# Selecting keys for the last four query blocks: in the projection, or beside the trunk

## The chip, the cores and the metric

One core of one Trainium2 chip runs the whole program. The metric is the device time of one execution in microseconds, as the median of several runs. The engines are called as in the profile: PE (TensorE, matmuls; PEld its weight loads), DVE (VectorE), ACT (ScalarE), POOL (GpSimd) and SP (SyncE, whose queue issues nearly all DMAs here).

## What is computed

A decoder layer with 2048 tokens and a width of 1024, in float32 (matmuls of full precision are made of three products of rounded halves). Three mixers work on columns of one projection, then an output projection, a norm, a gated feed-forward of width 2816 and a second norm:

```python
z = x @ w_in                      # columns split among the three mixers
# A: for each query, the 256 keys with the highest index score are attended to
rel   = relu(einsum('bqhd,bsd->bqhs', qi, ki) * IDX_DIM ** -0.5)
score = where(key_pos <= t, einsum('bqhs,bqh->bqs', rel, wi), -inf)
_, sel = top_k(score, 256)        # then softmax attention over sel
# B: differential attention, C: three dilated windows
x = LN(alpha * x + concat(A, B, C) @ w_o)
x = LN(alpha * x + (silu(x @ w_gate) * (x @ w_up)) @ w_down)
```

The change touches only where and when `sel` is found for the last of the sixteen blocks of 128 queries.

## The kernel before

The 2048 queries are 16 blocks of 128 (`NB`); groups `g` of 512 rows are the unit of the projection and of the trunk.

**Projection.** Four sections (two parts, two halves of the rows) run over chunks of 128 output columns. `chunk` makes a tile of 24 matmuls (`pj`, L543 to L545), ACT and DVE split it into halves `st` (L565 to L569), SP stores it. Value columns, with tokens down the rows, go through `natural` (`pnv`, `pnc`, L593 to L595). Weight pieces `w` are loaded by SP and split by ACT and POOL, the last six by ACT and DVE.

**Selection.** `index_work` handles two query blocks. It scores them against all earlier keys (for each 512 columns and each of four heads two matmuls `is`, L366 and L367, a relu on ACT, a multiply-add on DVE, L370 and L373), stores the scores, finds a threshold by 13 bisection passes (for even blocks on DVE, L399; for odd ones on ACT, L392), and finishes with a chain of a mask on ACT, some ten DVE instructions and one of POOL (L330) for each block. The result is a mask `sel` in DRAM. Width grows with the block: block 12 has 1664 columns, block 15 has 2048. The generators yield estimated costs for DVE, ACT, POOL and, while scoring, PE. In the projection `Background(2)` runs two of them at a time: `pump` is called between matmuls, advances them by planned time and keeps, in `free`, how long each of the three engines is taken. When five chunks are left, `bg.drain()` emits all that remains, and the pool `tk` with keys and scores is closed.

**`general_select`** then adds the flags of all blocks, loads the sum on every engine and branches: only if a flag was set, a slow exact selection runs. Nothing of it ran in the profile but the branch (L452). After it come the distance table of C and, with three chunks left, the loads of C's first head (`c_load`).

**Branch C with attention of group 0**, then the **trunk**. The trunk is woven of two streams. The main one is, for each group of 512 rows, `head` (transposes `mt`, output projection `wo`, norm, `xt`) and `body` (six rounds of gate `fg`, up `fu` and down `fd`, by `mm3`, L1215 to L1217; results to DVE, `sg`, `h`, `rT`). The side one is `all_attention`: attention of groups 1, 2 and 3 (A and B), then `head(3)`. Groups 2 and 3 are run A first, then B in one lane. Main group g starts after `ready` says that attention g has been emitted, and group 3's body needs all of `head(3)`. `weave` chooses who emits next: `due` rises by each cost of the side stream and falls by `share` times each cost of the main one; the side goes when `due` is below zero, or when the main stream sleeps. A yield's second number is a time to sleep in the planner's clock, which each cost of PE advances. PSUM in the trunk: three banks `f`, two `lg`, one `tr`, two `ac`. The order of emission is the priority; the framework fixes each engine's order when the program is built, and takes the branch as one indivisible unit.

Of the kernel before, what the change touches and what calls it, by code (L numbers as in the profile page):

```python
# [21 lines left out]
P = 128  # L22
# [17 lines left out]
OB2, UP_BUFS, CTB = 2, 4, 2  # L40
DRAIN, HEAD = 5, 3
C_EVAC = (1, 3)
LAM0 = 0.8 - 0.6 * math.exp(0.0)
# [23 lines left out]
C_SHARE = 0.2  # L67
T_SHARE = (0.45, 0.45, 0.45, 0.45)
T_AHEAD = 4.0
# [25 lines left out]
def tile_hybrid_layer(  # L95
# [212 lines left out]

    tk, close_tk = pool("tk", "right")
    kih = tk.tile([P, S], F32R, name="kih")  # L310
    kil = tk.tile([P, S], F32R, name="kil")
    dv = tk.tile([P, S], BF16, name="dumpv")
    da = tk.tile([P, S], BF16, name="dumpa")
    sign = tk.tile([P, S], BF16, name="sign")

    def index_keys(g):
        t0 = g * 512
        for dst, src in ((kih, kid[0]), (kil, kid[1])):
            load(dst[:, t0:t0 + 512].bitcast(F32), src[:, t0:t0 + 512])

# [16 lines left out]

    def index_work(blocks):


        n = len(blocks)
        q0 = blocks[0]
# [11 lines left out]
        for i, qb in enumerate(blocks):  # L354
# [5 lines left out]
            for c0 in range(0, w, 512):  # L360
                m = min(512, w - c0)
                acc = s_[:, c0:c0 + m]
                for h in range(4):
                    pt = bank("mm", f"is{qb}_{c0}_{h}")
                    q_ = qs[:, h, i * P:(i + 1) * P]
# [72 lines left out]

    def general_select():

        gp, close = pool("gp", "right")
        nf = gp.tile([P, 1], F32, name="nf")
        ones = gp.tile([P, 1], F32, name="ones")
        fi = gp.tile([1, 1], I32, name="fi")
        V.tensor_reduce(nf, flags, axis=AX.X, op=ALU.add)
        V.memset(ones, 1.0)
        pt = bank("ac", "nflags")
        PE.matmul(pt[:1, :1], nf, ones, start=True, stop=True)
# [3 lines left out]
        with tc.If(nc.values_load(fi[:1, :1]) > 0):  # L452
            for qb in range(2, NB):
                w = (qb + 1) * P
# [208 lines left out]
    def advance(loads, n):  # L663
        for _ in range(n):
            if loads:
# [3 lines left out]
                else:  # L669
                    xts[loads[0][0]] = tl  # L670

    xts = {}
    loads = [((0, g), read_x(0, g)) for g in range(2)]
    advance(loads, 5)
    for n, (part, half) in enumerate(sections):
        for pair in LISTS[part]:
            wts = None
            for g in (2 * half, 2 * half + 1):
# [4 lines left out]
                if pair == ("v",):  # L683
                    flush()
                    wts = wts or ws.take(3)
                    for tb, pt in enumerate(natural((3, 3, 2), 324, tl, f"v{g}", wts)):
# [7 lines left out]
                        store(vbd[:, b * P:(b + 1) * P, :].rearrange("h t d -> t h d"), vst.bitcast(F32))  # L694
                    for b0 in range(max(2, 4 * g), 4 * g + 4, 2):
                        bg.add(index_work([b0, b0 + 1]))
                    left -= 1
# [9 lines left out]
                else:  # L707
                    wts = wts or ws.take(len(pair))
                    for w_, what in zip(wts, pair):
                        chunk(w_, what, t0, tl)  # L710
                        left -= 1
                        last = n == 3
                        store_some(8 if last else 4)
                        if left == DRAIN:
                            bg.drain()
                            close_tk()
                            general_select()
                            cq, close_cq = pool("cq", "right")
                            ctab = c_distances(cq)
                            lambdas(cq)  # L720
                        if left == HEAD:
                            heads = {0: c_load(0)}
                        if what == 2:
                            flush()
                            index_keys(g)
                        advance(loads, 1)
# [687 lines left out]
    last, turns = [], [0]  # L1414

    def all_attention():

        for g in range(1, 4):
            yield from attention(g)
            ready[0] = g  # L1420
        hp, close_hp = pool("hp", "right")
        last.extend((hp, close_hp))
        last.append((yield from head(3, hp, Stream(hp, [w_o[dc] for dc in range(8)], 2, 2, "g"), iter(()), H_TAGS)))
# [77 lines left out]
```

## Time and profile before

| | us |
|---|---|
| median of 3 runs (3476.6 to 3488.01) | 3483.5 |
| the profiled execution | 3468.75 |
| its span, first to last instruction | 3467.0 |
| PE busy (mean granted clock 0.959 of full) | 3160.0 |
| DVE busy | 2148.0 |
| ACT busy | 1661.7 |
| POOL busy | 1020.6 |

The projection ends at about 695 us of the span, branch C at about 1160, the trunk's third body at about 3060; the last body runs alone to the end. Busy time of PE is the union of matmuls whose ends are modelled; a matmul of 512 columns is listed with 0.39 us, though one starts each 0.227 us in a dense stretch. A clock of 1.00 is the full one.

### The profile page before, as it was taken

Reading aid. Unit: us, or ns where it says so; the run is one execution under the profiler, and the core shown is the slowest. Engines: PE = TensorE matmul, PEld = TensorE weight load, DVE = VectorE, ACT = ScalarE, POOL = GpSimd, SP = SyncE. Lnnn points to the kernel's source line nnn. Section 1 sums busy time; section 2 is a strip of 40 time slices with the busy share of each in tenths; the row PEclk is TensorE's granted clock in tenths of the full one; section 3 lists DMA queues with packets and bytes.
Section 4 is the critical chain, followed back from the end, with each engine's and each line's share of the span. In section 5 each row is a group of like instructions: output and inputs, shape, how many; then the busy total and the mean of one; then the engine's idle time right before and its main releaser. Section 6 shows DMA issues by size and latency. Waiting matters only on the chain. (4 is left out here: it accounts for less than half of the span.)

```text
span 3467.0 us, 45777 instructions
## 1 busy us (share of the span) xinstructions
PE 3160.0 (91%) x15994; PEld 2601.1 (75%) x15994; DVE 2148.0 (62%) x5367; ACT 1661.7 (48%) x3113; POOL 1020.6 (29%) x591
## 2 busy tenths in 40 slices
PE   8998889869889799989988999999889999999997
PEld 7776667758878678877776777777678778778885
DVE  4979699547788567655468656465866555363224
ACT  3756656447666355545443445354444454232222
POOL 3221313014223123232223323321333332343332
PEclk9999999979999799999999999999999999999999
DMA  7453645588764633242244332422434242433322
GB/s 220 159 179 132 206 156 172 173 197 193 179 164 127 196 90 101 89 116 66 81 125 128 108 99 79 127 56 77 139 98 112 78 118 70 138 101 91 103 86 84
DMA packets 261241, 434.78 MB, mean 125 GB/s; under 512 B 49680, under 2 KB 149520, under 8 KB 256656
## 3 DMA queue, kind: packets, MB, share of 16 engines
q1 hardware_dynamic: 257808, 427.65, 42.4%
q0 software_dynamic: 1120, 3.67, 0.4%
q8 instruction: 126, 2.06, 0.2%
q14 instruction: 107, 0.88, 0.1%
q10 hardware_dynamic: 2080, 0.52, 0.1%
HBM read 331.65 MB, written 100.11 MB: 125 GB/s over the span
## 5 line engine op out<-in xcount | busy, mean ns | idle before, releaser
L155 POOL TENSOR_TENSOR f<-fr,f 128x1024 fp32r<-128x1024 f32 (+2 forms) x320 | 570.3, 1783 | 1400.6 <-ACT f L154 1314.4
L154 ACT CAST f<-fr 128x1024 fp32r<-128x1024 f32 (+2 forms) x392 | 321.4, 820 | 486.5 <-PE fd L1217 166.1
L1217 PE MATMUL fd<-h,f 128*128 128x512 f32 x704 | 280.7, 399 | 9.2 <-POOL f L155 9.0
L1215 PE MATMUL fd<-h,f 128*128 128x512 f32 x704 | 283.4, 403 | 3.1 <-ACT f L154 3.1
L1215 PE MATMUL fg<-xt,f 128*128 128x512 f32 x704 | 283.7, 403 | 0.7 <-ACT f L154 0.3
L1217 PE MATMUL fg<-xt,f 128*128 128x512 f32 x704 | 279.9, 398 | 3.4 <-DVE f L155 2.8
L1215 PE MATMUL fu<-xt,f 128*128 128x512 f32 x704 | 280.8, 399 | 1.4 <-ACT f L154 1.4
L1216 PE MATMUL fd<-h,f 128*128 128x512 f32 x704 | 279.9, 398 | 1.2 <-DVE h L155 1.2
L1217 PE MATMUL fu<-xt,f 128*128 128x512 f32 x704 | 278.4, 395 | 2.1 <-DVE f L155 1.2
L1216 PE MATMUL fg<-xt,f 128*128 128x512 f32 x704 | 280.0, 398 | 0.2 <-POOL xt L155 0.2
L1216 PE MATMUL fu<-xt,f 128*128 128x512 f32 x704 | 277.7, 394 | 0.0
L543 PE MATMUL pj<-xt,w 128*128 128x512 f32 x544 | 220.6, 406 | 25.6 <-ACT w L154 8.9
L545 PE MATMUL pj<-xt,w 128*128 128x512 f32 x544 | 217.8, 401 | 1.4 <-POOL w L155 1.4
L544 PE MATMUL pj<-xt,w 128*128 128x512 f32 x544 | 218.1, 401 | 0.7 <-POOL xt L155 0.7
L1022 ACT ACTIVATE c<-c,ob 128x256 f32<-128x256 f32 (+1 forms) x384 | 172.6, 451 | 66.4 <-DVE ob L1016 62.6
L1338 DVE TENSOR_TENSOR sg<-sg,fu 128x512 f32<-128x512 f32 x88 | 60.3, 686 | 228.3 <-PE fu L1217 227.6
L1352 DVE TENSOR_TENSOR rT<-rT,fd 128x512 f32<-128x512 f32 x160 | 109.3, 685 | 146.8 <-PE fd L1217 146.0
L1217 PEld LDWEIGHTS fd<-h,f 128*128 128x128 f32 x704 | 134.1, 190 | 41.5 <-POOL f L155 15.2
L155 POOL TENSOR_TENSOR w<-wr,w 128x1024 fp32r<-128x1024 f32 (+2 forms) x42 | 99.3, 2369 | 221.2 <-ACT w L154 200.9
L1217 PEld LDWEIGHTS fg<-xt,f 128*128 128x128 f32 x704 | 133.2, 189 | 33.0 <-DVE f L155 4.8
L1215 PEld LDWEIGHTS fd<-h,f 128*128 128x128 f32 x704 | 134.3, 191 | 30.2 <-ACT f L154 5.3
L1217 PEld LDWEIGHTS fu<-xt,f 128*128 128x128 f32 x704 | 132.3, 188 | 31.4 <-DVE f L155 2.8
(815 smaller groups left out, 8229.3 us busy)
## 6 DMA issues: line engine op xcount, KB each, us to landing
fr<-in_w_gate_dram SPq DMA_DIRECT2D x88, 512.0 KB
fr<-in_w_up_dram SPq DMA_DIRECT2D x88, 512.0 KB
fr<-in_w_down_dram SPq DMA_DIRECT2D x128, 256.0 KB
wr<-in_w_in_dram SPq DMA_DIRECT2D x42, 512.0 KB
fr<-in_w_o_dram SPq DMA_DIRECT2D x24, 512.0 KB
fr<-in_w_down_dram SPq DMA_DIRECT2D x64, 192.0 KB
ocd<-ob SPq DMA_DIRECT2D x16, 528.0 KB
ot<-ocd SPq DMA_DIRECT2D x32, 264.0 KB
```

The costliest lines, as they stand in the source:

```text
L154: A.copy(hi, src)
L155: lo_eng.tensor_tensor(lo, src, hi.bitcast(F32), op=ALU.subtract)
L543: PE.matmul(pt, wv[:, 0, k], tl[0][:, k], start=(k == 0), stop=False)
L544: PE.matmul(pt, wv[:, 0, k], tl[1][:, k], start=False, stop=False)
L545: PE.matmul(pt, wv[:, 1, k], tl[0][:, k], start=False, stop=(k == KC - 1))
L1022: A.activation(nl, nl, AF.Exp, bias=ob[:, place(blk), 64:65], scale=-1.0, accum_out=ob[:, place(blk), 65:66])
L1215: PE.matmul(pt, wv[:, 0, k], hi[:, k], start=(k == 0), stop=False)
L1216: PE.matmul(pt, wv[:, 0, k], lo[:, k], start=False, stop=False)
L1217: PE.matmul(pt, wv[:, 1, k], hi[:, k], start=False, stop=(k == n - 1))
L1338: V.tensor_tensor(sg, sg, pt, op=ALU.mult)
L1352: V.tensor_tensor(d, d, pt, op=ALU.add)
```

## The change

`LATER = 12`: the projection queues `index_work` only for blocks 2 to 11. Keys and buffers are made by a new `index_tiles`, once as `tk` for the projection, once as `lk` for the trunk. A generator `late_selection` loads the keys again from DRAM, makes two lanes (blocks 12 and 13; 14 and 15) and runs them in the side stream between attention 1 and attention 2; each lane sleeps for the longest of its engines' declared costs, and the PE cost of scoring counts in `due`. Its scoring takes PSUM banks `lg` and `ac` in place of `mm`. `general_select` is called twice, for blocks 2 to 11 at the old place, for 12 to 15 ahead of attention 3. The share of the side stream is 0.6 for groups 0 to 2.

```diff
+LATER = 12
-T_SHARE = (0.45, 0.45, 0.45, 0.45)
+T_SHARE = (0.6, 0.6, 0.6, 0.45)
...
-    def index_keys(g):
+    def index_tiles(name):
+
+        tk, close = pool(name, "right")
+        keys = [tk.tile([P, S], F32R, name=f"{name}{nm}") for nm in ("kih", "kil")]
+        dumps = [tk.tile([P, S], BF16, name=f"{name}{nm}") for nm in ("dumpv", "dumpa", "sign")]
+        return tk, keys, dumps, close
+
+    def index_keys(keys, g):
         t0 = g * 512
-        for dst, src in ((kih, kid[0]), (kil, kid[1])):
-            load(dst[:, t0:t0 + 512].bitcast(F32), src[:, t0:t0 + 512])
+        for p in range(2):
+            load(keys[p][:, t0:t0 + 512].bitcast(F32), kid[p][:, t0:t0 + 512])
...
-                    pt = bank("mm", f"is{qb}_{c0}_{h}")
+                    pt = bank(next(tags), f"is{qb}_{c0}_{h}")
...
-        V.tensor_reduce(nf, flags, axis=AX.X, op=ALU.add)
+        V.tensor_reduce(nf, flags[:, blocks[0]:blocks[-1] + 1], axis=AX.X, op=ALU.add)
...
-                    for b0 in range(max(2, 4 * g), 4 * g + 4, 2):
-                        bg.add(index_work([b0, b0 + 1]))
+                    for b0 in range(max(2, 4 * g), min(4 * g + 4, LATER), 2):
+                        bg.add(index_work([b0, b0 + 1], early, ("mm",)))
...
                             bg.drain()
-                            close_tk()
-                            general_select()
+                            early[-1]()
+                            general_select(range(2, LATER), "ac")
...
+    def late_selection():
+
+        tiles = index_tiles("lk")
+        for g in range(4):
+            index_keys(tiles[1], g)
+        lanes = [[0.0, index_work([b, b + 1], tiles, ("lg", "ac"))] for b in range(LATER, NB, 2)]
+        while lanes:
+            lane = min(lanes, key=lambda lane: lane[0])
+            if lane[0] > clock[0]:
+                yield 0.0, lane[0] - clock[0]
+                continue
+            r = next(lane[1], None)
+            if r is None:
+                lanes.remove(lane)
+            else:
+                cost = r[3] if len(r) > 3 else 0.0
+                lane[0] = clock[0] + max(cost, *r[:3])
+                yield cost, 0.0
+        tiles[-1]()
+
     def all_attention():
 
         for g in range(1, 4):
+            if g == 3:
+                general_select(range(LATER, NB), "ac")
             yield from attention(g)
             ready[0] = g
+            if g == 1:
+                yield from late_selection()
```

## Rows read from the trace of the kernel before

**Rows 1.** The page, part 1: busy us, share of the span, instructions.

```profile
PE 3160.0 (91%) x15994; PEld 2601.1 (75%) x15994; DVE 2148.0 (62%) x5367; ACT 1661.7 (48%) x3113; POOL 1020.6 (29%) x591
```

**Rows 2.** Windows: stretch, length, busy us and count by engine, clock, DMA, GB/s.

```profile
420.00:595.00 175.00, 158.04 (x654) 126.25 (x653) 162.95 (x234) 95.16 (x152) 45.58 (x17) 0.95 0.54 174
595.00:645.00 50.00, 47.05 (x207) 38.30 (x205) 16.70 (x25) 34.90 (x53) 0.00 (x0) 1.00 0.64 203
645.00:695.00 50.00, 40.75 (x170) 33.03 (x170) 40.36 (x43) 9.17 (x14) 7.92 (x2) 0.90 0.36 135
695.00:720.00 25.00, 4.70 (x22) 4.53 (x22) 6.03 (x26) 6.31 (x14) 5.10 (x6) 0.52 0.92 209
720.00:760.00 40.00, 28.51 (x187) 27.07 (x186) 18.18 (x93) 17.84 (x74) 4.31 (x3) 0.75 0.95 214
...
1180.00:3060.00 1880.00, 1774.52 (x8738) 1431.22 (x8737) 1132.29 (x2591) 875.14 (x1244) 571.79 (x320) 0.98 0.34 101
3100.00:3400.00 300.00, 299.26 (x1295) 242.58 (x1294) 80.40 (x95) 78.84 (x110) 103.48 (x62) 1.00 0.32 96
```

**Rows 3.** Groups of PE, 420 to 695 us: busy, mean ns, idle before, releasers.

```profile
L543 PE MATMUL pj<-xt,w 128*128 128x512 f32 x241 | 97.8, 406 | 10.0 <-DVE st L566 8.5 <-DVE sc L373 1.5
...
L593 PE MATMUL pnc<-w,xt 128*128 128x512 f32 x64 | 25.4, 397 | 0.0
```

**Rows 4.** Groups of DVE by shape, 420 to 695 us.

```profile
L399 DVE TENSOR_SCALAR_CACHE_REDUCE dumpv<-sc,xt 128x1664 bf16<-128x1664 f32 (+1 forms) x26 | 54.0, 2077 | 0.6
...
L569 DVE SCALAR_TENSOR_TENSOR st<-pj,st 128x512 fp32r<-128x512 f32 x15 | 10.3, 684 | 5.9 <-DMA v0e<-vcs 3.4 <-ACT st L568 1.3 <-DMA v1f<-vcs 1.3
L566 DVE TENSOR_TENSOR st<-pj,st 128x512 fp32r<-128x512 f32 x15 | 10.2, 682 | 6.9 <-ACT st L565 6.9
L155 DVE TENSOR_TENSOR xt<-xr,xt 128x1024 fp32r<-128x1024 f32 x4 | 7.7, 1916 | 0.0
L155 DVE TENSOR_TENSOR w<-wr,w 128x1024 fp32r<-128x1024 f32 x6 | 7.3, 1222 | 19.8 <-ACT w L154 19.8
...
L327 DVE TENSOR_TENSOR_SCAN fin<-fin 128x1536 f16<-128x1536 bf16 x1 | 3.3, 3349 | 0.0
...
L332 DVE TENSOR_SCALAR fin<-fin 128x1536 bf16<-128x1536 bf16 x1 | 0.6, 559 | 0.0
```

**Rows 5.** Waits of PE, 690 to 760 us: total us, times, longest.

```profile
PE c_0l L1004 <- DMA ckh<-kcd: 16.6, 1, 16.6
...
PE c_0l L1005 <- DMA ckl<-kcd: 3.7, 1, 3.7
```

**Rows 6.** Waits, the whole span: DVE at the branch.

```profile
DVE st L566 <- DVEq L452: 4.3, 1, 4.3
```

**Rows 7.** The chain that ended last, 2940 to 3065 us: start, us, what.

```profile
2950.68 1.96 DMA mixd<-ob
2952.71 3.43 DMA mx<-mixd
...
2963.01 6.37 DMA mx<-mixd
```

**Rows 8.** Timeline of ACT and DVE: start us, us, instruction.

```profile
433.89 0.59 ACT L565 CAST st<-pj 128x512 fp32r<-128x512 f32 x1 [2.58 <-PE pj L545]
436.43 2.10 DVE L428 SCALAR_TENSOR_TENSOR m<-iota,cntt,m 128x8 f32<-128x8 f32 x1
439.96 0.68 DVE L566 TENSOR_TENSOR st<-pj,st 128x512 fp32r<-128x512 f32 x1
...
653.18 0.23 DVE L428 SCALAR_TENSOR_TENSOR m<-iota,cntt,m 128x8 f32<-128x8 f32 x1
```

More of the change, by code (lines that the diff above doesn't have):

```diff
@@ L306, in tile_hybrid_layer @@
     bg = Background(2)
[L309 to L314, printed above, removed]
-    def index_keys(g):
+    def index_tiles(name):
[4 more added lines that the diff above has]
+    def index_keys(keys, g):
         t0 = g * 512
-        for dst, src in ((kih, kid[0]), (kil, kid[1])):
-            load(dst[:, t0:t0 + 512].bitcast(F32), src[:, t0:t0 + 512])
+        for p in range(2):
+            load(keys[p][:, t0:t0 + 512].bitcast(F32), kid[p][:, t0:t0 + 512])
     def select(full, w, t_, need, eq, pre, msk, dst):
@@ L336, in tile_hybrid_layer, with index_work @@
     scoring, finishing = [], []
-    def index_work(blocks):
+    def index_work(blocks, tiles, tags):
+        tk, (kih, kil), (dv, da, sign), _ = tiles
+        tags = itertools.cycle(tags)
         n = len(blocks)
@@ L437, in index_work, with general_select @@
             finishing.clear()
-    def general_select():
-        gp, close = pool("gp", "right")
+    def general_select(blocks, tag):
+        gp, close = pool(f"gp{blocks[0]}", "right")
         nf = gp.tile([P, 1], F32, name="nf")
@@ L444, in general_select @@
         fi = gp.tile([1, 1], I32, name="fi")
-        V.tensor_reduce(nf, flags, axis=AX.X, op=ALU.add)
+        V.tensor_reduce(nf, flags[:, blocks[0]:blocks[-1] + 1], axis=AX.X, op=ALU.add)
         V.memset(ones, 1.0)
-        pt = bank("ac", "nflags")
+        pt = bank(tag, f"nflags{blocks[0]}")
         PE.matmul(pt[:1, :1], nf, ones, start=True, stop=True)
@@ L452, in general_select @@
         with tc.If(nc.values_load(fi[:1, :1]) > 0):
-            for qb in range(2, NB):
+            for qb in blocks:
                 w = (qb + 1) * P
@@ L670, in advance @@
                     xts[loads[0][0]] = tl
+    early = index_tiles("tk")
     xts = {}
@@ L724, in tile_hybrid_layer @@
                             flush()
-                            index_keys(g)
+                            index_keys(early[1], g)
                         advance(loads, 1)
```

## The prediction

> **What bounds the kernel now.** I read the page first: TensorE (PE) is busy 91% of the span and VectorE (DVE) 62% [rows 1]. The kernel as a whole is bound by PE, so taking the selection away from the projection removes no PE work, it only moves it. A gain can come only from idle or slow-clocked PE time in the projection, a loss only from new idle time in the trunk. So next I read the windows by stage [rows 2]. From 420 to 595 us, where blocks 12 to 15 are scored and bisected, DVE is busy 163 of 175 us and PE 158; from 595 to 645 us most of that has ended and PE runs 207 matmuls in 50 us at a granted clock of 1.00; from 645 to 695 us the finishing of blocks 14 and 15 holds DVE, PE runs only 170. Then follows a hole, 695 to 720 us, with PE busy 4.7 of 25 us, and a slow start of branch C up to 760 us. The trunk (1180 to 3060 us) is different: PE 1775 of 1880 us, DVE 1132; there are only 105 us of idle PE to fill. Of group 3's body alone (3100 to 3400 us) PE is full and DVE has 80 of 300 us.
>
> **Part 1: the projection loses the four blocks.** What stays from 420 us on are 241 triples of `pj` and 64 of `pnc` matmuls [rows 3], 305 x 3 = 915. At the rate of the 595 to 645 us window, 50 / 207 = 0.2415 us each with that window's own idle time, they take 221 us, where now 275 us pass: 54 us gained. The upper bound is PE without any gap, 47.05 / 207 = 0.2273 us each, 208 us, a gain of 67. The lower end I take at 40: 8.5 us of stalls of `pj` are put down to a late copy on DVE [rows 3], but the weight loads stand in SP's queue behind the stores of `vc`, and these stay and are to be issued in less time. Blocks 8 to 11 remain, and block 11 ends early in this window, so DVE is not the limit after it.
>
> **Part 2: the hole before branch C.** `general_select` reads the flags of all blocks, and its branch stands on every engine; the last flag is written when block 15 is finished, so the loads of head 0 for C are issued only after it, and PE waits 16.6 us for `ckh` and 3.7 us more for `ckl` [rows 5]. With the flags of blocks 2 to 11 alone the branch is decided long before, `tk` is closed, and these loads go out three chunks before the projection ends. The most is 20.3 us; the least nothing, because the DMA engines are 92 to 95% busy from 695 to 720 and 720 to 760 us [rows 2] and the `vt` loads queue there anyway. By the tile sizes head 0 is 3.1 of some 11 MB loaded there (4.9 for `vt`, 3.1 for head 1), and SP and the DMA engines have room before 695 us (share 0.36), so I take 14. Parts 1 and 2: 68 us gained.
>
> **Part 3: the same PE work in the trunk.** Four blocks have 1664 + 1792 + 1920 + 2048 = 7424 columns, times four heads and two halves = 59392 columns, 116 matmuls of 512, at 0.2273 us: 26.4 us. PE has no free time there to speak of, so it counts in full, between 24 and 30.
>
> **Part 4: DVE while the late selection runs.** All of what the selection does on DVE moves too. DVE is busy 220 us between 420 and 695 us (the three windows of [rows 2]); less the projection's own `st` (10.3 + 10.2), `xt` 7.7, `w` 7.3, and less the finishing of block 11, seven instructions of 1536 columns with 12.9 us in sum, 171.6 us remain [rows 4], of which the bisection passes alone are 54.0. Now how long is the stretch in which the planner emits this? The side stream paces itself by the costs in the yields: scoring 24 + 26 us one after the other, 13 passes of 2.6 to 2.8 us, finishing of 27 and 31 us, the two lanes overlapping. Stepping `weave` through these costs, which gives an order and not a time, some 107 declared us of the main stream are put between first and last step. These are 107 / 0.64 x 3 = 502 matmuls, at 300 / 1295 us each [rows 2] 116 us, and they bring 0.268 us of DVE for each us [rows 2], 31 us. So PE has 116 + 26 = 142 us of work in this stretch and DVE 172 + 31 = 203 us: an excess of 61 us. The projection's `Background` kept account of what each engine already has; `late_selection` takes the longest engine of each lane by itself, so two lanes and the main stream may be emitted onto one DVE at a time. What is queued behind is the main stream: `sg` times `fu`, the low half of `h`, every `rT` addition, the hurried weight halves; and behind those, PE, with three banks of tag `f`. The lower bound is 0, if the main instructions slip between those of the lanes and the lanes fall behind without harm; the upper is 61 us, if DVE works in order. The nearest row is from the projection with its paced selection: a copy ready at 434.5 us got DVE at 440.0 us, 5.5 us late [rows 8]. A tile of the trunk takes 24 matmuls, 5.6 us, so such delays eat the spare banks but do not always stop PE. I take half, 30.5 us. ScalarE's share of the selection and some 20 DMAs on SP (key and query loads, stores of scores and masks) go by there too, in front of weight loads; ScalarE is busy 875 of 1880 us and DMA 0.34 in the trunk [rows 2], so I cost them at nothing while their cover holds, at up to 10 us if a store that waits for its mask holds up a weight load.
>
> A rule of the Trainium skill bears on this. The rows show a DVE instruction on 8 columns that takes 2.10 us at one place and 0.23 us at another [rows 8]. The Trainium skill, page "SBUF — State Buffer", section "SBUF: two separate sides", says that DVE and GpSimd share one port pair which an instruction with two SBUF inputs holds alone to its end; the trace agrees with that in kind, since the port's other user, POOL, splits weights in both stages. By the rule the late selection would lose more in the trunk, where POOL is busy 30% of the time [rows 2]: some 24 such instructions times 0.3 times about 1.2 us, an estimate of 9 us more, and the sum below would be 9 us higher.
>
> **Part 5: a second branch, and the tail.** The second `general_select` stops each engine once for the load of `fi` and the branch; DVE's wait there is 4.3 us now [rows 6], and I count it once, 4.3 us, between 1 and 8. In the order stepped so, the share of 0.6 puts attention 1's end earlier, at 286 instead of 314 of the planner's us, but attention 2 and 3 are held by their own waits, not by the share; so the side stream ends at 1701 instead of 1629 and group 2's body at 1632 instead of 1660. Today the end of the third body still fills PE under `head(3)`; after the change `head(3)` stands alone, 69.5 declared us with 52 of matmuls. What it then waits for is seen in the chain: 1.96 us store of `mixd`, 3.43 and 6.37 us loads of `mx` [rows 7], 11.8 us, and the norm behind it. I take the planner's 17.5, rounded to 18, between 8 and 28. The changed share by itself I cost at nothing (between -5 and +5).
>
> **Sum.** -54 - 14 + 26.4 + 30.5 + 4.3 + 18 = +11.2 us. The profiled execution took 3468.75 us (span 3467.0 and 1.75 around it): 3480.0 us for such an execution. The median of the runs shown is 3483.5 us, 14.8 above it; the difference is put on the median: 3494.7 us.
>
> **The rivals.**
> - *The cover holds*: DVE is busy 60% in the trunk [rows 2], the scheduler slips the main stream's short instructions in, and the side stream catches up. Part 4 is then about 5 us: -54 - 14 + 26.4 + 5 + 4.3 + 18 = -14 us, 3469 us. For it speaks that PE kept 90% while DVE stood at 93% from 420 to 595 us; against it that the emission there was paced by DVE and that a chunk needs DVE once in 24 matmuls, the trunk nearly twice as often. It decides when the excess of 61 us costs less than 19.
> - *DVE in order*: the lanes come first in emission, two chains take turns, and the main stream's instructions wait for both. Part 4 costs the full 61 us: +42 us, 3525 us. For it: no account is kept of DVE. Against it: chains leave gaps.
> - *The projection does not speed up*: the loads of weights behind the `vc` stores, not DVE, hold PE, and part 1 gives 25 us. Sum +40 us, 3524 us. Against it: 207 matmuls in 50 us with the same stores in the queue.
> - *It does not do what it says*: the flags still wait for something late, and the hole stays: +25 us, 3508 us. The diff closes the early tiles and asks for blocks 2 to 11 alone, so this is small.
>
> **How the numbers follow.** About 0.3% (10.5 us) is what a measurement of this kernel can tell from no change. Forecast (part 4 from 20 to 45 us, sum from 0 to +26) 0.45; cover holds 0.29, with sums from -35 to 0; DVE in order 0.13; no faster projection 0.09; hole stays 0.04. Faster by over 0.3%: two thirds and more of the cover case and little else from the bounds of parts 1 and 2, 0.24 + 0.06 = 0.30. Same: the rest of that case and the lower part of the forecast, 0.05 + 0.19 = 0.24. Slower: 0.46. The forecast's own range is 3482 to 3512 us; for 8 in 10 the range must take in most of the cover case, to -22 us, and the beginning of the two dear ones, to +44: 3462 to 3528 us.
>
> **What would show it.** In the changed profile: the last `pj` at about 641 us and the first `c_0l` within 8 us of it (parts 1 and 2); the `is` matmuls of the late blocks between some 1400 and 1700 us of the new span, DVE near full there, PE at 75 to 85% with a clock under 1.00, waiting for DVE's `rT`, `h` or `sg` (part 4); one branch between attention 2 and 3; and `wo` of `head(3)` with no `fg`, `fu` or `fd` beside it (part 5). PE over 93% in the late stretch would prove part 4 wrong, a last `pj` after 660 us part 1.

## The result and the profile after

The changed kernel takes 3537.35 us (median of 4 runs, 3528.01 to 3541.96) beside 3483.11 us for the kernel before on the same chip: a ratio of 1.0164, 95% interval 1.0149 to 1.0179. It is 54 us slower. The forecast was 3494.7 us with a range that ended at 3528; the sign was right, the size was not. All line numbers of the changed kernel lie one to four higher than before (`pj` is L546, the branch L455, the matmuls of the trunk L1219 to L1221, the halving helper L156).

The page of the changed kernel, its span, part 1 and the clock in 40 slices, to be held against [rows 1]:

```profile
span 3540.2 us, 45832 instructions
...
PE 3198.5 (90%) x15996; PEld 2615.6 (74%) x15996; DVE 2141.2 (60%) x5371; ACT 1641.7 (46%) x3097; POOL 1009.6 (29%) x591
...
PEclk9999999899997999888999999999989999889998
```

PE is busy 38 us longer than before, though the arithmetic is the same, and its share has fallen from 91 to 90%. A longer busy time for the same matmuls points to a lower clock; beside the start of the trunk (7 at 1062 to 1151 us) three slices of 8 stand in a row, from 1416 to 1682 us. So the next view is the windows by stage, as in [rows 2] (stretch, length, busy us and count of PE, PEld, DVE, ACT, POOL, then clock, DMA share, GB/s):

```profile
400.00:600.00 200.00, 199.56 (x881) 164.65 (x881) 46.87 (x57) 51.73 (x71) 43.74 (x21) 1.00 0.72 221
600.00:624.10 24.10, 24.10 (x108) 19.98 (x107) 6.19 (x15) 1.91 (x4) 4.35 (x3) 1.00 0.92 212
...
1078.90:1432.60 353.70, 323.24 (x1615) 263.05 (x1616) 229.22 (x616) 166.39 (x272) 91.08 (x49) 0.94 0.38 110
1432.60:1653.00 220.40, 168.28 (x587) 122.44 (x588) 203.84 (x282) 122.50 (x198) 58.07 (x28) 0.84 0.24 77
...
2250.00:2300.00 50.00, 41.05 (x199) 33.60 (x198) 18.88 (x41) 13.42 (x18) 10.79 (x7) 0.94 0.57 145
...
3057.70:3153.00 95.30, 75.66 (x321) 58.60 (x321) 47.40 (x109) 24.66 (x36) 30.86 (x15) 0.84 0.22 77
3153.00:3540.00 387.00, 363.97 (x1573) 292.89 (x1571) 120.67 (x150) 101.23 (x143) 131.29 (x77) 0.97 0.31 93
```

The first two rows are the projection's end: DVE is busy 47 of 200 us and PE 199.6 of 200 at a full clock, 881 matmuls, 0.227 us each. There is no gap left in it. The last `pj` ends at 624 us instead of 694, the first `c_0l` is at 627 instead of 712, and PE's only longer wait there is no longer one for a load:

```profile
PE c_0l L1008 <- DVE st L572: 2.6, 1, 2.6
```

The trunk begins (first `mt`) at 1078.9 us instead of 1167.6: 88.7 us gained. Then it loses 162: 2461 us long against 2299. The fourth row is the late selection, first `is` to last mask. In 220 us PE did 587 matmuls, 459 of them the main stream's (141 `fg`, 126 `fu`, 192 `fd`), was idle 52 us, and worked at a clock of 0.84, while DVE was busy 203.8 us, 92%. The waits of PE in that stretch (total us, times, longest):

```profile
PE fg L1221 <- DVE f L156: 8.8, 3, 4.2
PE fd L1219 <- ACT f L155: 8.5, 3, 5.6
PE fd L1219 <- DVE rT L1356: 8.1, 2, 5.6
PE is L369 <- DVE sc L376: 5.0, 5, 1.8
PE fd L1219 <- ACT h L155: 4.8, 1, 4.8
```

These are the waits that were named, DVE's `rT` and the halves of `h`, and also the halves of the weights, `f`. All rows of this view add up to 54 us: 29 of them end with DVE, 14 with ACT, 8 with POOL, 3 with a load. The 4.8 us for `h` lead back to DVE, since ACT itself had stood 11.5 us for `sg` of DVE. Of the 8.5 us for `f`, the longest wait, 5.6 us, follows on a row of ACT's own bisection passes (1516.8 to 1526.3 us) and a mask that waited 2.3 us for DVE. So the larger part of these waits is DVE's, but ACT, which was busy 122.5 of the 220 us, has a share of its own. How one of them looks is shown by the timelines of DVE, POOL and PE at one place (start us, us, instruction, then idle time and who ended it):

```profile
1534.85 1.89 DVE L427 SCALAR_TENSOR_TENSOR y<-lksign,sc 128x1664 f32<-128x1664 bf16 x1
...
1536.84 1.88 DVE L429 MAX8 m<-y 128x8 f32<-128x1664 f32 x1
1538.64 2.63 DVE L156 TENSOR_TENSOR f<-fr,f 128x1024 fp32r<-128x1024 f32 x1
```

```profile
1537.84 2.35 POOL L156 TENSOR_TENSOR f<-fr,f 128x1024 fp32r<-128x1024 f32 x1 [5.34 <-ACT f L155]
```

```profile
1531.20 0.80 PE L1219 MATMUL fd<-h,f 128*128 128x512 f32 x1 [5.57 <-ACT f L155]
...
1536.22 0.40 PE L1221 MATMUL fd<-h,f 128*128 128x512 f32 x1
1536.45 0.39 PE L1219 MATMUL fg<-xt,f 128*128 128x512 f32 x1
1536.68 0.40 PE L1220 MATMUL fg<-xt,f 128*128 128x512 f32 x1
1541.32 0.79 PE L1221 MATMUL fg<-xt,f 128*128 128x512 f32 x1 [4.25 <-DVE f L156]
1541.91 0.63 PE L1219 MATMUL fg<-xt,f 128*128 128x512 f32 x1
1542.34 0.63 PE L1220 MATMUL fg<-xt,f 128*128 128x512 f32 x1
```

PE has started the first two products of `fg` 0.23 us apart and needs the low half of a weight for the third. DVE does it only at 1538.64, after a pass of a lane and a `MAX8` of the other lane's finishing, and needs 2.63 us for it. PE stands for 4.25 us, and the matmuls behind the gap start 0.43 us apart, nearly twice as far as those just before it. The wait of 5.57 us that ended at 1531.20 was followed by the same slow spacing, until 1535.7. So a wait is paid twice here, once as idle time and again in the slow clock behind it. In all, the trace's record has the granted clock at half for 71.5 of the 220 us, and PE was busy in 55.5 of these, which makes some 28 us lost to the clock.

### The profile page after: what moved, and what is told of

It is laid out like the page before. It is cut to its first block, busy times and chain, and to the rows that moved or that the text cites. A ratio compares the mean times of both kernels' runs of the same rounds, so it can differ in the third digit from the quotient of the medians.

```text
span 3540.2 us, 45832 instructions
## 1 busy us (share of the span) xinstructions
PE 3198.5 (90%) x15996; PEld 2615.6 (74%) x15996; DVE 2141.2 (60%) x5371; ACT 1641.7 (46%) x3097; POOL 1009.6 (29%) x591
## 5 line engine op out<-in xcount | busy, mean ns | idle before, releaser
L156 POOL TENSOR_TENSOR f<-fr,f 128x1024 fp32r<-128x1024 f32 (+2 forms) x320 | 561.8, 1757 | 1471.6 <-ACT f L155 1358.3
L1219 PE MATMUL fd<-h,f 128*128 128x512 f32 x704 | 285.9, 407 | 22.4 <-ACT f L155 9.4
L1221 PE MATMUL fd<-h,f 128*128 128x512 f32 x704 | 282.8, 402 | 16.1 <-POOL f L156 15.8
L1221 PE MATMUL fg<-xt,f 128*128 128x512 f32 x704 | 283.5, 403 | 13.0 <-DVE f L156 9.8
L1219 PE MATMUL fu<-xt,f 128*128 128x512 f32 x704 | 283.6, 403 | 7.5 <-ACT f L155 4.9
L1219 PE MATMUL fg<-xt,f 128*128 128x512 f32 x704 | 286.0, 406 | 2.7 <-ACT f L155 1.9
L1221 PE MATMUL fu<-xt,f 128*128 128x512 f32 x704 | 281.0, 399 | 4.8 <-POOL f L156 3.6
L546 PE MATMUL pj<-xt,w 128*128 128x512 f32 x544 | 216.6, 398 | 15.6 <-ACT w L155 8.7
L548 PE MATMUL pj<-xt,w 128*128 128x512 f32 x544 | 215.3, 396 | 1.8 <-POOL w L156 1.4
L547 PE MATMUL pj<-xt,w 128*128 128x512 f32 x544 | 215.1, 396 | 0.7 <-POOL xt L156 0.7
L1219 PEld LDWEIGHTS fd<-h,f 128*128 128x128 f32 x704 | 135.4, 193 | 52.8 <-ACT f L155 13.9
L1221 PEld LDWEIGHTS fd<-h,f 128*128 128x128 f32 x704 | 134.9, 192 | 50.5 <-POOL f L156 24.1
L1221 PEld LDWEIGHTS fg<-xt,f 128*128 128x128 f32 x704 | 135.1, 192 | 44.0 <-DVE f L156 12.0
L1219 PEld LDWEIGHTS fu<-xt,f 128*128 128x128 f32 x704 | 134.3, 191 | 37.1 <-ACT f L155 7.8
L1221 PEld LDWEIGHTS fu<-xt,f 128*128 128x128 f32 x704 | 134.2, 191 | 35.2 <-POOL f L156 5.2
```

Source lines behind the costliest of these rows:

```text
L156: lo_eng.tensor_tensor(lo, src, hi.bitcast(F32), op=ALU.subtract)
L546: PE.matmul(pt, wv[:, 0, k], tl[0][:, k], start=(k == 0), stop=False)
L547: PE.matmul(pt, wv[:, 0, k], tl[1][:, k], start=False, stop=False)
L548: PE.matmul(pt, wv[:, 1, k], tl[0][:, k], start=False, stop=(k == KC - 1))
L1219: PE.matmul(pt, wv[:, 0, k], hi[:, k], start=(k == 0), stop=False)
L1221: PE.matmul(pt, wv[:, 1, k], hi[:, k], start=False, stop=(k == n - 1))
```

## Where the time went, in the prediction's own parts

From the two profiled executions (spans 3540.2 and 3467.0, 73.2 us apart; the medians are 54 apart). A matmul of the main stream is counted with 300 / 1295 = 0.2317 us from [rows 2], as in the prediction; in `head(3)` the matmuls of `fg`, `fu`, `fd` beside it are credited (159 before, 44 after). The window of `head(3)` runs from 10 us before its first `wo` to 35 us after its last; before the change it and the rest of the span were:

```profile
2967.00:3058.50 91.50, 89.51 (x423) 71.91 (x423) 35.05 (x72) 30.31 (x45) 33.56 (x20) 1.00 0.27 88
3058.50:3467.00 408.50, 382.49 (x1667) 307.84 (x1665) 145.63 (x203) 106.67 (x151) 140.73 (x81) 0.98 0.31 96
```

| part | forecast us | profiled us | how |
|---|---|---|---|
| 1 and 2, up to the trunk | -68 | -88.7 | 1078.9 - 1167.6 |
| 3 and 4, late stretch | +56.9 | +114.0 | 220.4 - 459 x 0.2317 |
| 5, tail `head(3)` | +18 | +30.4 | 95.3 - 91.5 + (159 - 44) x 0.2317 |
| 5, branch, and all the rest of the trunk | +4.3 | +17.5 | what remains of 73.2 |

Of the 114.0 us, 26.4 are the selection's own PE work (part 3). That leaves 87.6 for part 4, forecast at 30.5 with 61 as the most: 52.1 us of idle time, and 35.5 us by which PE's busy time of 168.3 is longer than 106.3 + 26.4. Some 28 of the 35.5 are the clock, as counted above; the rest isn't located (in part a matmul beside a gap is listed with its whole 0.4 to 0.8 us, and not with the 0.23 us to the next start).

## Experiments

The kernel before ran beside each group of runs (3475 to 3481 us); ratios go by that. Where nothing else is said the edit is to the changed kernel.

### The three pieces apart

The share alone, in the kernel before (`share_only`), and the share put back in the changed one (`share_old`):

```diff
-T_SHARE = (0.45, 0.45, 0.45, 0.45)
+T_SHARE = (0.6, 0.6, 0.6, 0.45)      # share_only; share_old is the reverse
```

> The kernel before with a share of 0.6 and nothing moved. Theory: the share costs little by itself, within 8 us of 3483 us. Rival (the share crowds the trunk): 3510 to 3525 us.

> The changed kernel with the side stream's share back at 0.45. Theory (the loss is made where the late selection fills VectorE: 203.8 of 223 us busy, PE 170): the stretch keeps its form, the time stays within 10 us of the changed kernel's 3537 us, 3527 to 3550. Rival (the higher share crowds attention 1 and 2 and costs some 40 us in all): 3490 to 3510 us, and the 353 us from the first mt to the first late is fall to about 320.

Measured: `share_only` 3501.4 us, 1.0072 (1.0053 to 1.0090), 25 us slower; `share_old` 3551.73 us, 1.0214 (1.0189 to 1.0239), slower still than the changed kernel. Both theories missed. The share isn't free in either kernel, and it has opposite signs in them. In the kernel before it costs 25 us; in the changed one taking it back costs 14 more (17 by the ratios).

To place the 25 us, the new share beside group 0 of the trunk alone, in the kernel before:

```diff
+T_SHARE = (0.6, 0.45, 0.45, 0.45)
```

> Edit: the kernel before with T_SHARE = (0.6, 0.45, 0.45, 0.45), so the new share beside group 0 of the trunk alone (attention 1). Theory (the 25 us of the share alone are lost while attention 1 is pressed into less main work: PE 91 us of 100 there against 98): most of them here too, ratio 1.004 to 1.008. Rival (attention 2 and 3 lose them): ratio 0.998 to 1.002.

Measured: 3498.87 us, 1.0058 (1.0041 to 1.0075): 20 of the 25 us come with group 0, so with attention 1. Two windows in it, first of the kernel before, then with the share:

```profile
1300.00:1400.00 100.00, 98.19 (x504) 81.01 (x503) 73.53 (x183) 56.70 (x89) 28.86 (x15) 1.00 0.34 98
1400.00:1500.00 100.00, 98.61 (x494) 80.90 (x493) 64.56 (x165) 57.25 (x85) 27.02 (x15) 1.00 0.28 83
```

```profile
1300.00:1400.00 100.00, 93.37 (x487) 75.05 (x486) 78.39 (x199) 51.32 (x85) 25.74 (x14) 0.99 0.30 87
1400.00:1500.00 100.00, 96.54 (x468) 79.08 (x468) 58.73 (x138) 45.85 (x69) 25.77 (x15) 0.99 0.28 83
```

PE falls from 196.8 to 189.9 of 200 us where more of attention 1 is put beside less main work. These 7 us are shown; where the other 13 arise isn't.

The late selection left out (`no_late`: that part of the computation is missing, and attention 3 reads masks of block 11 for blocks 12 to 15, by an edit of the load that isn't printed here), and the second branch left out (`no_branch2`):

```diff
-            if g == 1:
-                yield from late_selection()
```
```diff
-            if g == 3:
-                general_select(range(LATER, NB), "ac")
```

> The changed kernel without the late selection: blocks 12 to 15 take block 11's mask (that part of the computation is left out, the output changes), all else stays. Theory: the 223 us of the late stretch hold 468 matmuls of the main stream, 106 us at the dense rate, so some 115 us go away there, and head(3) no longer stands alone at the end (another 15 to 30 us): 3390 to 3425 us. Rival (the loss lies in the share, the branch and the pool changes, spread over the trunk): only the 26 us of scoring and a part of the stretch go, 3470 to 3500 us.

> The changed kernel without the second branch (the exact selection for blocks 12 to 15, which no flag asks for here, is left out). Theory: the branch costs its own stop, 4 to 9 us: 3528 to 3535 us. Rival (as an indivisible unit it also cuts the streams' prefetch, and the slow stretch from 2500 to 2600 us is its echo): 3505 to 3520 us.

Measured: `no_late` 3416.06 us, 0.9829 (0.9803 to 0.9855), as expected. So, in us of the kernel before: the share +25, from there to `no_late` -85 (the lighter projection, the second branch included), and from there to the changed kernel +117, which is the late selection. `no_branch2` 3514.8 us, 1.0115 (1.0083 to 1.0146): 17 us for the branch, four times what was put down, and a time in the rival's range. In `no_late` the end of the side stream looks as it did before the change:

```profile
2833.30:2925.40 92.10, 88.18 (x415) 70.87 (x414) 36.99 (x73) 30.63 (x43) 36.41 (x20) 0.98 0.32 103
2925.40:3413.70 488.30, 460.01 (x1996) 370.58 (x1994) 166.20 (x230) 126.50 (x182) 163.93 (x100) 0.98 0.31 93
```

In its 92.1 us `head(3)` has 143 `fg`, `fu` and `fd` beside it, and 1996 matmuls are left when it ends. In the changed kernel only 1573 are left, no more than group 3's own body (1584 `fg`, `fu` and `fd`). That number is the **cover** still in hand. It tells where `head(3)` stands alone: 1570 to 1573 are left in the changed kernel, `share_old`, `booked_only`, `branch_mid`, `no_branch2`, `later14_mid` and `later14_old`. It doesn't put the runs in order: `share_only`, 25 us slower than the kernel before, has 1990 left, and `short_waits`, the slowest but two, 2527.

### DVE in the late stretch

Three cures of the excess, two of them with the waits of attention 2 and 3 shortened, so that `head(3)` isn't alone; and the shortened waits by themselves:

```diff
-LATE = (1.0, 1.0, 1.0, 1.0)
+LATE = (1.0, 1.0, 0.8, 0.8)          # short_waits, one_lane, booked
```
```diff
-lanes = [[0.0, index_work([b, b + 1], ...)] for b in range(LATER, NB, 2)]
+lanes = [[0.0, itertools.chain(*(index_work([b, b + 1], ...) for b in range(LATER, NB, 2)))]]   # one_lane
```
```diff
-                lane[0] = clock[0] + max(cost, *r[:3])
+                end = clock[0] + cost                       # booked
+                for e, t in enumerate(r[:3]):
+                    if t:
+                        free[e] = max(free[e], clock[0]) + 1.35 * t
+                        end = max(end, free[e])
+                lane[0] = end + 0.1
```
```diff
-        for it in range(STEPS):
+        for it in (range(STEPS) if q0 < LATER else (0, STEPS - 1)):   # few_passes, old waits
```

> The changed kernel with the planner's waits inside attention 2 and 3 at 0.8 of their length, so that head(3) is emitted beside the third body again and not alone. Theory (what is lost outside the late stretch is lost chiefly where head(3) stands alone, 26 us idle between 3050 and 3160 us at a clock of 0.81): 20 to 35 us less than the changed kernel's 3537, 3502 to 3517 us. Rival (denser emission of attention crowds VectorE and takes it back): 3530 to 3550 us.

> As the run with short waits, and the two lanes of the late selection one after the other instead of side by side. Theory (two lanes and the main stream are emitted onto one VectorE): VectorE is asked for some 216 us of work over 189 us of matmuls instead of 203 over 142, so half of the loss goes: 30 to 45 us less than the run with short waits. Rival (the loss comes with each us of selection on VectorE, however it is spread): within 12 us of the run with short waits.

> As the run with short waits, two lanes, but late_selection books each lane's times on engines that both share, with 0.35 added for the main stream. Theory: the stretch grows to 250 us or more, PE is busy over 92% of it at a clock near 1.00, and 45 to 70 us go against the run with short waits. Rival (port contention with POOL or the order on DVE costs the same however it is paced): within 15 us of it.

> The changed kernel with two bisection passes instead of thirteen for blocks 12 to 15 (11 of 13 passes and the two flag instructions of these blocks are left out, so their masks are wrong). It takes 57 of 172 us from VectorE's part of the late selection and 63 us from ScalarE's. Theory: the stretch shrinks by the 57 us and some clock, 3465 to 3490 us. Rival (the matmuls, loads and pool changes of the late selection make the loss): 3515 to 3535 us.

Measured: `short_waits` 3561.36 us, 1.0248 (1.0231 to 1.0265), slower by 24 to 29 us though PE idles only 2.5 us in `head(3)` there, so the tail isn't the loss to cure first; neither range had it. Against it `one_lane` takes 39 us off (3522.18, 1.0131, 1.0114 to 1.0148) and `booked` 58 (3503.3, 1.0070, 1.0054 to 1.0087), both as expected. The late stretch in `one_lane`, `booked` and `few_passes`:

```profile
1432.40:1681.10 248.70, 213.24 (x857) 166.07 (x857) 225.73 (x301) 139.24 (x221) 82.34 (x40) 0.92 0.28 90
```

```profile
1435.20:1681.20 246.00, 208.46 (x837) 162.74 (x838) 224.26 (x301) 139.26 (x221) 78.70 (x40) 0.93 0.29 91
```

```profile
1426.00:1586.10 160.10, 124.71 (x471) 92.03 (x472) 146.77 (x176) 62.33 (x101) 43.17 (x20) 0.90 0.25 83
```

In the first two the stretch is 26 to 28 us longer than in the changed kernel, but 250 to 270 more matmuls go by in it, the idle time is 36 to 38 us instead of 52, and the clock 0.92 to 0.93 instead of 0.84. DVE's work is nearly the same but for the extra main work. PE stays at 85%, under the 92% expected of `booked`. `few_passes` (blocks 12 to 15 bisected in 2 passes of 13 and without their two flag instructions, so their masks are wrong) is 3504.07 us, 1.0080 (1.0062 to 1.0099): with 57 us of DVE work less, 30 us of 117 come back, less than expected; the stretch is 160.1 us with PE idle for 35.4, and DVE is still busy 92% of it. By the measure of the table (length, less the main matmuls at 0.2317 us, less 26.4) the stretch costs 53 us in `one_lane`, 55 in `booked` and 54 in `few_passes`, instead of 87.6. So it is shown three times that the selection's work on the engines beside PE is a cause of the loss. That it is DVE's work alone isn't shown: `one_lane` and `booked` spread ACT's passes too, and `few_passes` takes 63 us from ACT with the 57 from DVE. For DVE speak its 92% against ACT's 56% in the changed kernel, and the larger part of the waits above.

### The same account with the old waits

> Edit: the changed kernel, where late_selection only keeps account of DVE, ACT and POOL: a step of a lane is put behind what the other lane has been given on the same engine, each step with 1.35 times its declared cost (the rest being left to the main stream). Waits of attention unchanged. Theory (the excess of DVE work in the late stretch is what the change costs): the gain of the booking is that of the run with shorter waits, 40 to 58 us off 3537: 3480 to 3497 us, PE busy over 83% of the stretch with a clock over 0.90. Rival (the booking helped there only because the shorter waits had crowded the attention around it): under 15 us gained, 3522 to 3537 us.

Measured: 3600.04 us, 1.0353 (1.0318 to 1.0387). That is 63 us slower than the changed kernel, where 40 to 58 us faster was expected and under 15 by the rival, and 97 us slower than `booked`, from which only the waits of attention differ. The stretch itself is as good as in `booked` (first row below; by the table's measure it costs 54.5 us). The loss lies elsewhere, and these windows and groups of PE show where:

```profile
1429.80:1675.20 245.40, 209.66 (x838) 164.66 (x839) 223.62 (x301) 139.59 (x221) 78.15 (x40) 0.93 0.29 91
2320.00:2390.00 70.00, 26.61 (x94) 18.85 (x93) 28.21 (x85) 11.01 (x18) 16.01 (x8) 0.56 0.50 142
3020.00:3120.00 100.00, 60.68 (x199) 39.90 (x196) 50.69 (x138) 29.97 (x43) 1.48 (x1) 0.58 0.12 41
```

```profile
L857 PE MATMUL b_14o<-b_14T,vb 128*128 128x256 f32 (+1 forms) x32 | 12.6, 496 | 6.5 <-ACT b_14T L155 5.5
L829 PE MATMUL b_1l<-bk,bq 128*128 128x512 f32 (+3 forms) x16 | 10.8, 687 | 2.8 <-DVE b_13m L831 1.5 <-DVE b_12m L831 0.7
...
L1247 PE MATMUL mt<-ident,mx 128*128 128x128 f32 x24 | 5.9, 427 | 12.2 <-DMA mx<-mixd 10.2 <-DVE mt L156 1.9
```

At 2320 to 2390 and 3020 to 3120 us PE has 26.6 of 70 and 60.7 of 100 us of work, at clocks of 0.56 and 0.58. None of it is `fg`, `fu`, `fd` or `wo`: only attention (`b_14o`, `b_1l`) and transposes. The main stream has finished its group and sleeps until the next attention is emitted. The late selection, now dense, had used up 250 more matmuls of the main stream, and these were missing beside attention 2 and 3. Main work is a stock that is spent once. A dense late stretch is worth something only if the rest of the side stream needs less of it, as with the waits at 0.8.

### Half the dose

`LATER = 14`: two blocks return to the projection, one lane remains.

```diff
-LATER = 12
+LATER = 14
```

> Edit: the changed kernel with LATER = 14: blocks 12 and 13 are selected in the projection again, 14 and 15 (3968 of the 7424 columns, one lane) in the trunk. Theory (two lanes at a time on one DVE make the loss): one lane has some 92 us of DVE work over a longer time than it needs, so its cost in the trunk is near its PE work and some waiting, 35 to 45 us above the run without any late selection (3416 us), and the projection gives back 25 to 40 us of what it gained: 3476 to 3501 us. Rival (the loss goes in proportion to the columns, 53% of 121 us): 3416 + 64 + 25 to 40: 3505 to 3520 us.

Measured: 3490.28 us, 1.0043 (1.0022 to 1.0064). That is in the range of the theory. By the ratios 42 us come back for 47% of the columns, though the projection gives up 40 us of its gain (first `mt` at 1119.1 us). So the two blocks that remain cost some 34 us (3490 - 3416 - 40), where 53% of 117 would be 62: one lane is far cheaper than half of two. Then, with it, the old share (`later14_old`), and the old share with the waits of attention 2 and 3 at 0.9 (`later14_old_short`):

> Edit: the changed kernel with LATER = 14 and T_SHARE = 0.45 throughout. Theory (cover: with 0.45 more main work is used up beside attention 1 and is missing at the end of the side stream, as with four late blocks, where 0.45 was 14 us slower): 3495 to 3515 us, head(3) with no fg, fu, fd of group 2 beside it and PE idle there near 20 us. Rival (0.6 presses attention 1, as in the kernel before, where it lost 20 to 25 us): 3462 to 3478 us.

> Edit: as later14_old, with the waits of attention 2 and 3 at 0.9, so that the side stream needs less cover. Theory (attention 1 at the old pace loses nothing, shorter waits give the cover back, no bare stretch): 3465 to 3485 us, PE idle under 6 us beside head(3). Rival (any shortening of the waits crowds the attention, as 0.9 left body 3 alone for 446 us in the run with the moved branch): 3495 to 3510 us.

Measured: `later14_old` 3525.96 us, 1.0153 (1.0133 to 1.0173), more than the theory of cover asked for; `later14_old_short` 3467.42 us, **0.9982** (0.9966 to 0.9997), as expected. One number of the plan, the waits at 0.9, is worth 58 us. The end of the side stream in `later14_old` (30 us around the start of `head(3)`, then `head(3)`):

```profile
3010.00:3040.00 30.00, 13.31 (x67) 10.40 (x66) 10.82 (x34) 6.61 (x12) 0.00 (x0) 0.67 0.44 153
3033.60:3128.80 95.20, 75.94 (x323) 59.06 (x323) 47.35 (x109) 26.46 (x37) 30.20 (x15) 0.84 0.23 77
```

and in `later14_old_short`, the `head(3)` and what follows it:

```profile
2978.90:3070.40 91.50, 89.97 (x425) 72.29 (x424) 35.04 (x72) 30.30 (x45) 33.58 (x20) 1.00 0.28 88
3070.40:3477.80 407.40, 380.98 (x1666) 306.73 (x1665) 145.98 (x203) 106.79 (x151) 140.10 (x81) 0.98 0.32 96
```

In the first, the 30 us around its start are more than half empty, `head(3)` idles 19.3 us at 0.84, and the matmuls of `fg` and `fu` in it are only those of group 3 that follow it. In the second `head(3)` is full, at a clock of 1.00, with 161 `fg`, `fu` and `fd` beside it, and 1666 matmuls are left at its end, as in the kernel before (1667). Beside this tail, 19 us of idle time less were found in the part of the trunk ahead of `head(3)` (128.7 against 147.9). `later14_old_short` is the only version with the whole computation that isn't slower than the kernel before; its gain of 0.2% can hardly be told from nothing.

### The place of the branch

The second `general_select` between A and B of attention 2, in five kernels:

```diff
             close_tp()
+            if g == 2:
+                general_select(range(LATER, NB), "ac")
             tp, close_tp = pool(f"bp{g}", "right")
...
-            if g == 3:
-                general_select(range(LATER, NB), "ac")
```

The kernel of `later14_mid` holds one edit more than its text says: the account of `booked` is in it as well. It isn't in `later14_mid_short`.

> Edit: the changed kernel with the second general_select put between branches A and B of attention 2, where the buffers of A are given up and those of B taken, instead of ahead of attention 3. Theory (the second branch costs some 20 us since the loads of attention 3 can't be issued before it): at the new place fewer loads stand behind it, they wait for buffers of A anyway; 10 to 20 us gained, 3517 to 3527 us, and attention 3's first loads are issued before its predecessor's end. Rival (the stop of all engines itself costs that much, wherever it stands): 3532 to 3542 us.

> Edit: the changed kernel with both edits, the account of the shared engines in late_selection and the second general_select between A and B of attention 2. Theory (two separate losses): the gains add, 50 to 75 us off 3537: 3462 to 3487 us. Rival (both are one and the same loss of time in the middle of the trunk, so the second edit gives nothing once the first is there): within 5 us of the run with the account alone.

> Edit: the changed kernel with the account of the shared engines, waits of attention 2 and 3 shortened to 0.8 and the second general_select between A and B of attention 2. Theory (cover: the account uses up main work, the shorter waits need less of it, so no stretch of attention is bare, and the branch then costs its 18 us by place alone): 3503 - 18, 3478 to 3492 us, no window of 25 us between 1700 and 2900 without fg, fu, fd or wo. Rival (the moved branch gave 18 us only where the waits were long; with the account it gave nothing): 3498 to 3508 us.

> Edit: the changed kernel with LATER = 14 and the second general_select between A and B of attention 2. Theory (the branch costs about 18 us by its place ahead of attention 3's loads, whatever the number of blocks before it): 3490 - 18, 3465 to 3480 us. Rival (with half of the late work the branch is covered): within 5 us of 3490.

> Edit: as later14_mid, and the waits of attention 2 and 3 at 0.9. Theory (cover is nearly enough with two late blocks, head(3) idles 11 us there; shorter waits have little to win and crowd the attention): between 5 us faster and 15 us slower than later14_mid. Rival (cover still binds): 10 to 25 us faster than later14_mid.

Measured: `branch_mid` 3519.54 us, 1.0132 (1.0092 to 1.0172), 11 us less, as expected, but its interval reaches into that of the changed kernel; `booked_mid` 3599.45 and `booked_short_mid` 3502.84, both within 1 us of the same kernels with the branch at its old place, which are the rivals; `later14_mid` 3529.52, 1.0141 (1.0119 to 1.0163), 39 us slower than `later14`, which neither theory had; `later14_mid_short` 3507.53, 1.0085 (1.0068 to 1.0101), 22 us faster than that. In `later14_mid` `head(3)` idles 20.1 us and 1571 matmuls are left after it, in `later14` 11.4 us and 1583. But these 39 us belong to the moved branch and the account together, and the 22 us to the shorter waits and the leaving-out of the account together, so neither can be put down to the branch or to cover. The account alone cost 63 us in `booked_only`; whether it is the cause here too isn't shown. What is left on the branch alone is 17 us for leaving it out, and 11, 0 and 0 us for moving it. In the changed kernel its direct waits are small (total us, times, longest):

```profile
PE a_0l L829 <- DMA aq<-qad: 8.7, 1, 8.7
...
DVE f L156 <- DVEq L455: 4.4, 1, 4.4
```

DVE stands 4.4 us, as it did at the single branch [rows 6], and PE then waits 8.7 us for a query load of attention 3 that was issued only behind the branch. In `no_branch2` the same wait is 3.6 us, so 5 of the 17 us are found here; the rest isn't located.

## Why the prediction was wrong

**Parts 1 and 2** named the right causes and were too small, 68 us against 88.7. The rate taken included a window's own gaps; without the selection there are none, and the last `pj` at 624 us is beyond the upper bound given for part 1 (a gain of 67; it was 70). The bound began at 420 us, and by then the lighter projection was already ahead: 1504 of its matmuls were done instead of 1487, some 4 us. The waits for `ckh` and `ckl` are gone altogether (20.3 us [rows 5], 14 taken); a wait of 2.6 us for `st` stands in their place.

**Part 3**, 26.4 us, is taken over as it was: the 128 `is` matmuls are those counted, but their time can't be measured apart from the waits around them.

**Part 4 is the step that failed.** DVE's work in the stretch was worked out as 172 + 31 = 203 us and measured at 203.8, the main stream's matmuls as 502 and measured at 459; PE at 75 to 85% is 76%. The step that turned 61 us of excess into "half, 30.5 us" was wrong, and so was its upper bound. Measured are 87.6 us, 57 more than forecast, of 62 by which the profiled times missed (73.2 against 11.2). The bound let the stretch be as long as DVE's work; it was 220 us, with DVE at 92%. It took PE's work at the full clock, though [rows 2] had a clock of 0.52 and 0.75 where PE starved; at 0.84, PE's busy time alone grew by 35.5 us, some 28 of them by the clock. ScalarE's share was put at nothing, and 14 of PE's 54 us of waits there end with ACT. And the row the half rested on, a copy 5.5 us late [rows 8], was read as a delay that spare banks absorb; here the delayed result was a weight half or an `rT` for which PE stood at once. The rival with DVE in order, 3525 us, was the nearest of those written down, and by its own price still short.

**Part 5.** `head(3)` stands alone, as forecast; 18 us were put down, 30.4 measured, beyond the end at 28. PE's longest wait there is for the norm, not for the loads:

```profile
PE xt L1296 <- DVE r L1292: 7.7, 1, 7.7
```

The branch was put at 4.3 us, the wait that its row showed; without it the kernel is 17 us faster. A row that shows one engine's wait at a branch doesn't show what stands behind the branch, and here it was the first query load of an attention.

**The share** was put at nothing, -5 to +5 us. It costs 25 us in the kernel before and gains 14 in the changed one. The prediction did step the order and saw that the side stream ends later and the main one sooner, by 72 and 28 of the planner's us, but made of it only the tail. What `booked_only` and the pair `later14_old` and `later14_old_short` show is that this balance is the larger quantity: 97 and 58 us from the waits alone.

One rule was weighed: the Trainium skill, page "SBUF — State Buffer", section "SBUF: two separate sides", lets a DVE instruction with two SBUF inputs wait for a GpSimd one. The rows above agree in kind: the weight half took DVE 2.63 us beside a POOL instruction that ran from 1537.84 for 2.35 us. In the late stretch such halves took 2180 ns, between 1700 and 2250 us 1222 ns (groups of DVE by shape, busy us, mean ns):

```profile
L402 DVE TENSOR_SCALAR_CACHE_REDUCE lkdumpv<-sc,xt 128x1920 bf16<-128x1920 f32 x13 | 28.7, 2204 | 0.1
L402 DVE TENSOR_SCALAR_CACHE_REDUCE lkdumpv<-sc,xt 128x1664 bf16<-128x1664 f32 x13 | 25.2, 1935 | 0.0
...
L156 DVE TENSOR_TENSOR f<-fr,f 128x1024 fp32r<-128x1024 f32 x4 | 8.7, 2180 | 0.0
...
L156 DVE TENSOR_TENSOR h<-sg,h 128x512 fp32r<-128x512 f32 x6 | 5.7, 956 | 0.3 <-ACT h L155 0.3
...
L330 DVE SCALAR_TENSOR_TENSOR fin<-fin,needt 128x1792 bf16<-128x1792 f16 x1 | 4.1, 4079 | 0.0
...
L330 DVE SCALAR_TENSOR_TENSOR fin<-fin,needt 128x2048 bf16<-128x2048 f16 x1 | 2.3, 2340 | 0.0
```

```profile
L156 DVE TENSOR_TENSOR f<-fr,f 128x1024 fp32r<-128x1024 f32 x15 | 18.3, 1222 | 10.2 <-ACT f L155 8.5 <-PE b_10t L848 1.6
```

Four weight halves 0.96 us longer make 3.8 us of DVE time. Other instructions with two SBUF inputs were longer beside POOL too: one half of `h` took 2.31 us where the other five took 0.69, L330 took 4.08 us on 1792 columns and 2.34 on 2048, one product with `hmask` 1.36 us where three took 0.28. That is 8.5 us in all, near the 9 us that the rule was estimated at. They didn't lift DVE's sum above the forecast, 203.8 against 203 us, perhaps since the rows that the 172 us come from have such instructions as well (the 2.10 us of [rows 8]). Three instructions with one SBUF input (L324 and L333, `fin`) were 0.9 to 2.2 us longer beside POOL; the rule as cited doesn't cover them. The bisection passes, one SBUF input each, make 53.9 us of DVE's time.

**What stays open**: why shorter waits by themselves (`short_waits`) lose 24 us or more with PE idle 105 us in the middle of the trunk; where 13 of the share's 20 us in group 0 arise; where 12 of the branch's 17 us arise; what the moved branch costs with one lane, where it was tried only together with another edit; how the loss of the late stretch is divided between DVE and ACT; and how much of the 17.5 us in the last row of the table is the branch and how much the share.

## What to carry to other kernels

When work moves from a stage that waits to a stage that is full, sum it for each engine over the stretch in which it will be emitted, and where one engine's sum exceeds PE's, reckon with the whole excess, and with PE's slower clock on top of it; here 61 us of excess became 87.6. Where a long side stream is hidden behind a main one, count the main stream's work as a stock: what is spent beside the new piece is missing beside the last one, and how many matmuls are left when the side stream ends tells whether its last piece stood alone. A pause or a share in the plan that was right before such a move has to be set anew after it; here that was worth more than the move.

## What the runs showed that was not expected

A gap of 4.25 us in a stream of full matmuls was followed by matmuls that start 0.43 us apart instead of 0.23, and over a starved stretch the granted clock was 0.84, in the bare ones 0.56 and 0.58. A stretch with 15% idle time (`booked`) kept 0.93. Of the 87.6 us lost in the late stretch, some 28, a third, were the clock.
